# Router logits taken from the residual sums, and the last two tiles of an output projection one after the other

## The chip, the cores and the metric

The kernel runs on one core of a Trainium2 chip. The number that counts is the device time of one execution in microseconds (us): 1569.45 as the median of three runs (1567.67 to 1571.55). The profile is of one more execution, of 1567.72 us.

Five engines work side by side, each through its own queue of instructions, in order, waiting on the others by semaphores: TensorE (PE, matrix products and transposes), VectorE (DVE), ScalarE (ACT), GpSimd (POOL) and SyncE (SP). SP and POOL also issue the transfers between memory and the core.

## What is computed

One encoder layer for 1024 tokens of width 1024, in float32: a token mixer (attention and pooling, merged by gates, with an output projection), a residual sum with layer norm, a mixture of 32 experts of which each token takes two, and a second residual sum with layer norm. The part that matters here:

```
x   = layer_norm(ALPHA * x + merged @ w_out, ln1_gain, ln1_bias)      # 1024 x 1024
g   = x @ w_router_group  + b_router_group                            # 1024 x 4, top 1
e   = x @ w_router_expert + b_router_expert                           # 1024 x 32, top 2 in the group
out = layer_norm(ALPHA * x + sum of two experts, ln2_gain, ln2_bias)
```

An expert is a gated MLP: `(silu(x @ gate) * (x @ up)) @ down`.

## The kernel before

Products are made in three passes of a faster format (`mm3`, lines 161 to 164: high by high, high by low, low by high), so each 128x512 product is three matmul instructions. Around the change there are two stages.

**The output projection.** The 1024 tokens are 8 tiles of 128 rows (0 to 7). `begin` loads a tile's input rows (POOL, line 919) and takes two PSUM banks. A *step* is one call of `mix`: one `k` of eight for one half `n` of the columns, three matmuls (`pw`). After the eight steps of a half, `residual` (lines 931 and 932, VectorE) adds the input and takes the sums for mean and variance; after the second half `norm` (line 936) applies the layer norm in place (`layer_norm`, lines 785 to 798) and writes the rows to memory as `X1`, from which the experts gather.

Between the steps stands the routing of earlier tiles: `turn` (TensorE transposes the rows, `px`; ScalarE copies them, `xT`; POOL scales the rows by ALPHA, line 945, and writes them to `Y`, onto which the experts' results are added), `route` (logits by 8 products against `wr`, line 820, then the choice of group and experts by some 30 small VectorE operations up to `Ms`, line 857), `weights`, `places` (two small products give each token its place in its experts' lists, lines 879 and 880; then one-hots, `ohr`, line 890) and `place` (the one-hots multiplied into the table `first` by two products, line 898). Where each goes is written by hand: `S5` names for each group of tiles the step before which a piece is put, and `S5_END` what comes behind the last step. Tiles 0 and 1 run side by side (a half of 0, a half of 1, and so on), 2 to 5 singly, 6 and 7 side by side. For TensorE and ScalarE this order of the program is kept; VectorE and POOL are ordered by a scheduler.

**The experts.** When all tiles are in the table, VectorE makes the row numbers (`rows_at`, lines 1013 and 1014), POOL gathers rows of `X1` for the first four experts (line 1089), and then TensorE runs through 32 experts. Their weights, 192 pieces of 1 MB, are loaded by SP (line 1048) as soon as one of 15 slots (and a sixteenth buffer) comes free, the first ones during the output projection.

Of the kernel before, what the change touches and what calls it, by code (L numbers as in the profile page):

```python
# [11 lines left out]
F32 = mybir.dt.float32  # L12
# [3 lines left out]
AF = mybir.ActivationFunctionType  # L16
OP = mybir.AluOpType
# [6 lines left out]
D = 1024  # L24
# [30 lines left out]
MEAN_LAG = 1  # L55
B = tuple(2300.0 + 550.0 * i for i in range(8))
FR = (0.5, 0.25, 0.25)
S5_LATE = ((32, "turn", 6),)
S5 = {
    1: (),  # L60
    2: ((13, "turn", 0), (15, "route", 0)),
    3: ((1, "turn", 1), (3, "route", 1), (8, "places", 0), (11, "turn", 2), (13, "place", 0), (13, "route", 2), (14, "places", 1)),
    4: ((2, "place", 1), (4, "places", 2), (10, "turn", 3), (10, "place", 2), (12, "route", 3)),
    5: ((3, "places", 3), (10, "turn", 4), (10, "place", 3), (12, "route", 4)),
    7: ((3, "places", 4), (10, "turn", 5), (10, "place", 4), (12, "route", 5), (21, "places", 5), (26, "place", 5)) + S5_LATE,
}
S5_END = (("logits", 6), ("route", 6), ("turn", 7), ("weights", 6), ("logits", 7), ("route", 7), ("places", 6), ("weights", 7), ("place", 6), ("places", 7), ("place", 7))
Y_OUT = (6, 7)
COMB = ()
M4 = 4  # L70
# [6 lines left out]
C_IOTA, C_FREQ, C_RCNT, C_P, C_DOWN, C_PAY, C_N = 128, 224, 225, 241, 242, 250, 314  # L77


P_GB, P_SUB, P_PS, P_N = 0, 16, 17, 21  # L80


def constants():
# [23 lines left out]
def body(tc, ctx, A, out):  # L107
# [32 lines left out]
    def tiny(shape, name, dt=F32, bufs=2):  # L140
        return (ph["S2"] if "S2" in ph else sm).tile([128] + shape, dt, name=nm(name), tag="t_" + name, bufs=bufs)
# [640 lines left out]
    ps5 = tc.tile_pool(name="ps5", reuse_waits="tile", bufs=1, space=PSUM)  # L782
    p5 = ps5.__enter__()

    def layer_norm(tiny, x, bs, y, g, b):

        mv = tiny([2], "mv")
        DVE.bn_aggr(mv, bs)
        v = tiny([4], "v")
        DVE.tensor_scalar(v[:, 0:1], mv[:, 1:2], EPS, None, op0=OP.add)  # L790
        steps = rsqrt_steps(v[:, 1:2], v[:, 0:1], v[:, 2:3])
        steps[0]()
        DVE.scalar_tensor_tensor(x, x, mv[:, 0:1], g, op0=OP.subtract, op1=OP.mult)
        steps[1]()
        steps[2]()
        DVE.tensor_scalar(v[:, 1:2], v[:, 1:2], -5.0 / 16, None, op0=OP.mult)
        for c in (slice(0, 512), slice(512, 1024)):
            DVE.scalar_tensor_tensor(y[:, c], x[:, c], v[:, 1:2], b[:, c], op0=OP.mult, op1=OP.add)

    wr = ph["S2"].tile([128, 8, 36], F32, name="wr")  # L800
    br = ph["S2"].tile([128, 36], F32, name="br")
    SP.dma_start(wr, A["wr"])
    SP.dma_start(br, bass.AP(tensor=A["br"].tensor, offset=0, ap=[[0, 128], [1, 36]]))

    down8, slots = cst[:, C_DOWN:C_DOWN + 8], cst[:, C_IOTA:C_IOTA + CAP]
    scat = []

    def turned(x):
        xT1 = raw4([8, 128], "xT1")
        for g in range(2):  # L810
            px = p5.tile([128, 4, 128], F32, name=nm("px"), tag="X", bufs=2)
            for k in range(4):
                PE.transpose(px[:, k], x[:, (4 * g + k) * 128:(4 * g + k) * 128 + 128], ident)
            ACT.copy(xT1[:, 4 * g:4 * g + 4], px)
        return xT1

    def logits(xT1):
        pr = p5.tile([128, 512], F32, name=nm("pr"), tag="R", bufs=2)
        for k in range(8):
            PE.matmul(pr[:, :36], xT1[:, k], wr[:, k], start=k == 0, stop=k == 7)  # L820
        lg = tiny([36], "lg")
        DVE.tensor_add(lg, pr[:, :36], br)
        return lg, pr

    def route(j, lg, pr):
# [103 lines left out]
    def residual(j, n):  # L929
        c, x = slice(n * 512, n * 512 + 512), tl[j]["x"]  # L930
        DVE.scalar_tensor_tensor(x[:, c], x[:, c], ALPHA, tl[j]["w"][n], op0=OP.mult, op1=OP.add)
        DVE.bn_stats(tl[j]["s"][:, 6 * n:6 * n + 6], x[:, c])

    def norm(j):
        x = tl[j]["x"]
        layer_norm(tiny, x, tl[j]["s"], x, *lnp)
        POOL.dma_start(X1[j * 128:j * 128 + 128], x)

    def step(what, j):

        if what == "turn":
            x = tl[j]["x"]
            tl[j]["t"] = turned(x)
            y = slot2([D], F32, "yy") if j in Y_OUT else x
            POOL.tensor_scalar(y, x, ALPHA, None, op0=OP.mult)
            POOL.dma_start(Y[j * 128:j * 128 + 128], y)
        elif what == "route":
            if "l" not in tl[j]:
                tl[j]["l"] = logits(tl[j]["t"])
            tl[j]["m"] = route(j, *tl[j]["l"])  # L950
            if j < 6:
                weights(j, *tl[j]["m"][3:])
        elif what == "logits":
            tl[j]["l"] = logits(tl[j]["t"])
        elif what == "weights":
            weights(j, *tl[j]["m"][3:])
        elif what == "places":
            tl[j]["p"] = places(j, *tl[j]["m"][:3])
        else:
            place(j, *tl[j]["p"])  # L960
            if j < 6:
                store_rows(j)


    with tc.manual_schedule(engines={mybir.EngineType.PE, mybir.EngineType.Activation}):
        for group in ((0, 1), (2,), (3,), (4,), (5,), (6, 7)):
            for j in group:
                begin(j)
            todo = list(S5[group[-1]])
            i = 0  # L970
            for n in range(2):
                for j in group:
                    for k in range(8):
                        while todo and todo[0][0] <= i:
                            step(*todo.pop(0)[1:])
                        mix(j, k, n)
                        i += 1
                    if i == 32:
                        for s_ in todo:
                            step(*s_[1:])  # L980
                    residual(j, n)
                    if n:
# [338 lines left out]
def arrange(x, positions, w_in, gate_bias, lam_vecs, subln_gain, w_pool, pool_scale, w_branch_a, w_branch_b, w_out,  # L1321
# [87 lines left out]
```

## Time and profile before

| | |
|---|---|
| median of three runs | 1569.45 us (1567.67 to 1571.55) |
| the profiled execution | 1567.72 us, of which the span of the profile is 1565.9 us |
| busy: PE, DVE, ACT, POOL | 95%, 76%, 60%, 17% of the span |
| output projection, first to last product issued | 809.4 to 921.5 us |
| first gather of the experts | 940.5 us |
| mean granted clock of TensorE | 0.977 of full speed |

Times in a trace count from the start of the span. A matmul's duration includes its way through the pipeline, so back-to-back matmuls overlap; what one costs is read from one start to the next. What stands in brackets at the end of a row is how long the engine was idle before it, and on whom it waited.

### The profile page before, as it was taken

To read this page: it belongs to the slowest core of one execution; us is meant where nothing else is said; L and a number is where in the kernel's file an instruction comes from. 1 tells how busy PE (TensorE), PEld (TensorE's weight loads), DVE (VectorE), ACT (ScalarE), POOL (GpSimd) and SP (SyncE) were. 2 spreads that over 40 slices of the span, in tenths; PEclk is the share of its full clock that TensorE was granted. 3 is DMA by queue.
4 is the path that set the end of the run, shared out by engine and by line. 5 is a ranking of instruction groups with operands and counts; after the bars stand their busy time and mean duration, and the time that the engine had idled before them with its cause. 6 is when DMAs were issued, how large, how long until landed. Compare 5 with 4: busy or idle time off the path is not lost.

```text
span 1565.9 us, 22004 instructions
## 1 busy us (share of the span) xinstructions
PE 1489.4 (95%) x7627; PEld 1190.3 (76%) x7627; DVE 1195.5 (76%) x2284; ACT 945.7 (60%) x1571; POOL 270.0 (17%) x231
## 2 busy tenths in 40 slices
PE   8999999999999999999999987999999999999980
PEld 6988887798798898888888865777777777777750
DVE  5774224987988987775566787999999999899967
ACT  4323124666666666674341125888888888888864
POOL 0001000220210211100002543223222222222110
PEclk9999999999999999999999988999999999999995
DMA  7156223746856755618465568999999999999935
GB/s 235 59 172 203 78 80 96 222 160 168 225 185 182 208 186 145 155 60 315 153 259 196 203 228 291 360 367 378 374 377 370 364 365 364 360 347 368 399 118 215
DMA packets 116977, 375.46 MB, mean 240 GB/s; under 512 B 13767, under 2 KB 44871, under 8 KB 91504
## 3 DMA queue, kind: packets, MB, share of 16 engines
q1 hardware_dynamic: 76128, 303.25, 52.8%
q0 software_dynamic: 40160, 69.96, 17.3%
q8 instruction: 61, 1.00, 0.2%
q10 hardware_dynamic: 576, 0.83, 0.2%
q14 instruction: 52, 0.43, 0.1%
HBM read 312.44 MB, written 69.78 MB: 244 GB/s over the span
## 4 chain that ended last, share of the span: by engine, by line
PE 54%; issue 29%; POOL 9%; DVE 5%; ACT 2%; DMA 2%; POOLq 0%; DVEq 0%; SPq 0%; ACTq 0%
POOL Y L1101 7%; PE ps L570 4%; PE pg L162 4%; PE pg L163 4%; PE pg L164 4%; PE po L621 3%; POOL xg L1089 2%; PE pa L162 2%; PE pa L164 2%; PE pa L163 2%; PE pv L162 2%; PE pv L164 2%; PE tp L606 2%; PE pv L163 2%; PE pw L162 2%
## 5 line engine op out<-in xcount | busy, mean ns | idle before, releaser
L148 DVE TENSOR_TENSOR wh<-we,wh 128x1024 fp32r<-128x1024 f32 x384 | 460.4, 1219 | 57.3 <-ACT wh L147 53.3
L147 ACT CAST wh<-we 128x1024 fp32r<-128x1024 f32 x384 | 401.4, 1046 | 93.4 <-PE gu L164 61.8
L162 PE MATMUL gu<-wh,xT 128*96 128x512 f32 x512 | 204.8, 400 | 1.9 <-ACT xT L147 1.9
L164 PE MATMUL gu<-wh,xT 128*96 128x512 f32 x512 | 203.5, 397 | 0.8 <-DVE xT L148 0.8
L163 PE MATMUL gu<-wh,xT 128*96 128x512 f32 x512 | 202.3, 395 | 0.0
L1101 POOL DMA_INDIRECT Y<-y,idx x32 | 104.6, 3268 | 271.8 <-ACT y L1109 267.0
L148 DVE TENSOR_TENSOR w<-wraw,w 128x512 fp32r<-128x512 f32 x111 | 75.8, 686 | 93.5 <-ACT w L147 93.0
L147 ACT CAST w<-wraw 128x512 fp32r<-128x512 f32 x111 | 68.5, 621 | 115.9 <-PE pg L164 36.4
L573 ACT ACTIVATE P<-ps,stat 128x256 f32<-128x256 f32 (+7 forms) x128 | 94.8, 741 | 59.2 <-DVE stat L572 58.8
L164 PEld LDWEIGHTS gu<-wh,xT 128*96 128x96 f32 x512 | 83.3, 163 | 37.3 <-DVE xT L148 1.5
L162 PEld LDWEIGHTS gu<-wh,xT 128*96 128x96 f32 x512 | 83.4, 163 | 35.3 <-ACT xT L147 2.3
L163 PEld LDWEIGHTS gu<-wh,xT 128*96 128x96 f32 x512 | 83.6, 163 | 34.3 <-issue 0.2
L162 PE MATMUL dn<-wh,hT 128*96 128x512 f32 x256 | 102.5, 400 | 0.6 <-ACT hT L147 0.6
L164 PE MATMUL dn<-wh,hT 128*96 128x512 f32 x256 | 101.0, 395 | 0.0
L570 PE MATMUL ps<-K,Q 128*128 128x512 f32 (+2 forms) x384 | 99.6, 365 | 1.2 <-DVE z L461 0.8
L163 PE MATMUL dn<-wh,hT 128*96 128x512 f32 x256 | 100.6, 393 | 0.0
L162 PE MATMUL pg<-xT,w 128*128 128x512 f32 x256 | 100.5, 393 | 0.0
L163 PE MATMUL pg<-xT,w 128*128 128x512 f32 x256 | 100.1, 391 | 0.0
L164 PE MATMUL pg<-xT,w 128*128 128x512 f32 x256 | 100.0, 391 | 0.0
L572 DVE TENSOR_REDUCE stat<-ps 128x1 f32<-128x256 f32 (+7 forms) x128 | 95.4, 747 | 1.1
L570 PEld LDWEIGHTS ps<-K,Q 128*128 128x128 f32 x384 | 64.7, 189 | 10.8 <-DVE z L461 1.3
L162 PE MATMUL pv<-w,xT 128*128 128x256 f32 x256 | 72.9, 285 | 0.0
(277 smaller groups left out, 3390.6 us busy)
## 6 DMA issues: line engine op xcount, KB each, us to landing
we<-in_we_dram SPq DMA_DIRECT2D x192, 1024.0 KB, 21.7
wraw<-in_w_dram SPq DMA_DIRECT2D x61, 512.0 KB, 3.9
Q<-RQ POOLq DMA_DIRECT2D x64, 256.0 KB, 4.8
RQ<-rh SPq DMA_DIRECT2D x32, 256.0 KB, 3.2
K<-RK POOLq DMA_DIRECT2D x16, 512.0 KB, 4.4
V<-RV POOLq DMA_DIRECT2D x16, 512.0 KB, 5.6
OT<-ohl SPq DMA_DIRECT2D x48, 128.0 KB, 2.4
oT<-OT POOLq DMA_DIRECT2D x6, 1024.0 KB, 10.3
```

The source lines that it names most:

```text
L147: ACT.copy(hi, src)
L148: DVE.tensor_sub(lo, src, r(hi))
L162: PE.matmul(ps, a[0], b[0], start=start, stop=False)
L163: PE.matmul(ps, a[0], b[1], start=False, stop=False)
L164: PE.matmul(ps, a[1], b[0], start=False, stop=stop)
L570: PE.matmul(ps[:, c:c + n], q[:, o, m, qc], Kt[h, m][:, c:c + n], start=o == 0, stop=o == 1)
L572: DVE.tensor_reduce(st_[:, m:m + 1], ps[:, :W], AX.X, OP.max, negate=True)
L573: ACT.activation(Pt[h, i][m][:, :W], ps[:, :W], AF.Exp, bias=st_[:, m:m + 1], accum_out=st_[:, 2 + m:3 + m])
L606: PE.transpose(ps[:, k], p[:, (4 * g + k) * 128:(4 * g + k) * 128 + 128], ident)
L621: PE.matmul(o[:, 0, c], Vt[h][:, a, kt], aT[kt // 4][:, kt % 4, b, c], start=j == 0, stop=j == len(parts) - 1)
L1089: q = POOL.indirect_dma_start(out=x, out_offset=None, in_=X1, in_offset=IO(ap=idx[:, int(e < NXG), expert[e]:expert[e] + 1], axis=0), boun ...
L1101: q = POOL.indirect_dma_start(out=Y, out_offset=IO(ap=idx[:, 0, expert[e]:expert[e] + 1], axis=0), in_=y, in_offset=None, bounds_check=T - ...
```

## The change

The layer norm of a row is a subtraction of its mean, a product with its root and with the gains, and the biases. A logit is linear in that, so it can be had from the residual sum itself: the product of the sum with router rows multiplied by the gains, less the mean times the column sums of these rows, times the root, plus the column sums of the router rows multiplied by the biases.

- Ahead of the projection POOL fills 128x128 ones (in one of the 15 slots) and makes from each of the eight 128x36 blocks of `wr` one times the gain and one times the bias (`w72`); the gains and biases, by column, come with the small parameter block `par`. A new step `router` has TensorE multiply the ones by these 72 columns, in eight products, put before step 8 of tiles 0 and 1; VectorE takes the two sums over (`wc`, `br`).
- ScalarE scales the row of gains by -5/16 once, instead of a VectorE operation for each tile.
- `turn` transposes the residual sum; `norm`, the write of `X1`, the scaling and the write of `Y` come after it. `stats` makes mean and root; `logits` uses them in two VectorE operations in place of one.
- Tiles 6 and 7 run one by one; `S5` and `S5_END` are new. The first half of tile 7's turn is put before step 10 of its own projection, the second behind it.

The diff, without most of the tables (a name that is not defined in it stands in the kernel above):

```diff
-S5_LATE = ((32, "turn", 6),)
-    7: ((3, "places", 4), (10, "turn", 5), (10, "place", 4), (12, "route", 5), (21, "places", 5), (26, "place", 5)) + S5_LATE,
+    7: ((3, "turn", 6), (5, "place", 5), (6, "route", 6), (10, "half", 7), (15, "places", 6)),
...
-    def layer_norm(tiny, x, bs, y, g, b):
...
+    ACT.activation(lnp[0], lnp[0], AF.Copy, scale=-5.0 / 16)
...
+    wgb = slot([704], F32, "wgb")
+    w72, ones = wgb[:, :576].rearrange("p (k n) -> p k n", k=8), wgb[:, 576:]
+    POOL.memset(ones, 1.0)
+    for k in range(8):
+        g, b = (par[:, P_LN + 8 * i + k:P_LN + 8 * i + k + 1] for i in range(2))
+        POOL.tensor_scalar(w72[:, k, :36], wr[:, k], g, 5.0 / 16, op0=OP.mult, op1=OP.mult)
+        POOL.tensor_scalar(w72[:, k, 36:], wr[:, k], b, None, op0=OP.mult)
+    POOL.tensor_copy(wr, w72[:, :, :36])
+
+    def router():
+
+        pr = p5.tile([128, 512], F32, name=nm("pr"), tag="R", bufs=2)
+        for k in range(8):
+            PE.matmul(pr[:, :72], ones, w72[:, k], start=k == 0, stop=k == 7)
+        DVE.tensor_copy(wc, pr[:, :36])
+        DVE.tensor_add(br, br, pr[:, 36:72])
...
-        DVE.tensor_add(lg, pr[:, :36], br)
+        mean, root = tl[j]["r"]
+        DVE.scalar_tensor_tensor(lg, wc, mean, pr[:, :36], op0=OP.mult, op1=OP.subtract)
+        DVE.scalar_tensor_tensor(lg, lg, root, br, op0=OP.mult, op1=OP.add)
...
+    def stats(j):
+
+        mv, v = tiny([2], "mv"), tiny([3], "v")
+        DVE.bn_aggr(mv, tl[j]["s"])
+        DVE.tensor_scalar(v[:, 0:1], mv[:, 1:2], EPS, None, op0=OP.add)
+        for s_ in rsqrt_steps(v[:, 1:2], v[:, 0:1], v[:, 2:3]):
+            s_()
+        tl[j]["r"] = mv[:, 0:1], v[:, 1:2]
+
     def norm(j):
         x = tl[j]["x"]
-        layer_norm(tiny, x, tl[j]["s"], x, *lnp)
+        mean, root = tl[j]["r"]
+        DVE.scalar_tensor_tensor(x, x, mean, lnp[0], op0=OP.subtract, op1=OP.mult)
+        for c in (slice(0, 512), slice(512, 1024)):
+            DVE.scalar_tensor_tensor(x[:, c], x[:, c], root, lnp[1][:, c], op0=OP.mult, op1=OP.add)
         POOL.dma_start(X1[j * 128:j * 128 + 128], x)
+        y = slot2([D], F32, "yy") if j in Y_OUT else x
+        POOL.tensor_scalar(y, x, ALPHA, None, op0=OP.mult)
+        POOL.dma_start(Y[j * 128:j * 128 + 128], y)
...
+        elif what == "turn":
+            for g in range(int(j == 7), 2):
+                turn(j, g)
+            if j < 7:
+                norm(j)
...
-        for group in ((0, 1), (2,), (3,), (4,), (5,), (6, 7)):
+        for group in ((0, 1), (2,), (3,), (4,), (5,), (6,), (7,)):
...
                     if n:
-                        norm(j)
+                        stats(j)
```

What the change moves, at three places. On TensorE, at the end of the projection of before (`px`: transposes, of tile 6 and then of tile 7; `pr<-wr`: logits; `pr<-Ms`: places; `pr<-ohr`: place):

```order
L164 MATMUL pw_9100<-wo_8147,mg_8063 128x512
L813 MATMUL px_9350<-cst,xx_9092 128x128 x4
L813 MATMUL px_9356<-cst,xx_9092 128x128 x4
L820 MATMUL pr_9382<-wr,xT_9349 128x36 x8
L813 MATMUL px_9426<-cst,xx_9097 128x128 x4
L813 MATMUL px_9432<-cst,xx_9097 128x128 x4
L820 MATMUL pr_9453<-wr,xT_9425 128x36 x8
L879 LDWEIGHTS tri
L879 MATMUL pr_9382<-Ms_9423,tri 128x32
```

and of the changed kernel (`pr_9364` is tile 6's, `pr_9501` tile 7's):

```order
L888 MATMUL pr_9364<-Ms_9406,tri 128x32
L889 LDWEIGHTS one
L889 MATMUL pr_9364<-cum,one 128x32
L163 MATMUL pw_9309<-wo_8147,mg_8063 128x512
L164 MATMUL pw_9309<-wo_8147,mg_8063 128x512
L165 MATMUL pw_9309<-wo_8147,mg_8063 128x512
L821 MATMUL px_9486<-cst,xx_9306 128x128 x4
L907 MATMUL pr_9364<-ohr_9458 96x64 x2
L827 MATMUL pr_9501<-wr,xT_9434 128x36 x8
L888 LDWEIGHTS tri
L888 MATMUL pr_9501<-Ms_9550,tri 128x32
```

Tile 6's turn, logits and places now stand ahead of the last projection products; behind them are half a turn, tile 6's place and tile 7.

On VectorE, in the tile 3 group, ahead of the one-hots of tile 1 (`ohr_8697`), with the routing of tile 2 (`t`, `M`, `s`) around them, before:

```order
L852 TENSOR_REDUCE mx_8654<-big_8668 128x4
L888 SCALAR_TENSOR_TENSOR pt_8705,at_8698<-M_8543,pr_8505 128x32
L841 TENSOR_TENSOR t_8657<-big_8668,mx_8654 128x32
L865 SCALAR_TENSOR_TENSOR eq_8680,s_8648<-mx_8654,G_8652 128x4
L890 TENSOR_SCALAR ohr_8697<-cst,at_8698 128x96
L842 TENSOR_TENSOR t_8657<-t_8657,cst 128x32
L890 TENSOR_SCALAR ohr_8697<-cst,at_8698 128x96
L846 TENSOR_REDUCE f_8655<-t_8657 128x4
```

and now (`ohr_8714`):

```order
L855 TENSOR_REDUCE f_8667<-t_8669 128x4
L880 TENSOR_SCALAR s_8660<-s_8660 128x1
L897 SCALAR_TENSOR_TENSOR pt_8722,at_8715<-M_8529,pr_8490 128x32
L856 TENSOR_TENSOR oh_8668<-t_8669,f_8667 128x32
L881 RECIPROCAL s_8660<-s_8660 128x1
L899 TENSOR_SCALAR ohr_8714<-cst,at_8715 128x96
L864 TENSOR_TENSOR M_8687<-G_8664,oh_8668 128x32
L882 TENSOR_TENSOR cst<-s_8660 128x1
L899 TENSOR_SCALAR ohr_8714<-cst,at_8715 128x96
L866 TENSOR_TENSOR Ms_8690<-M_8687 128x32
```

The one-hots have moved from the middle of tile 2's routing to its end, one row ahead of its result `Ms_8690`.

On VectorE behind the last projection product, tile 7 (`xx_9306` are its rows, `lg_9510` its logits), in the changed kernel:

```order
L940 SCALAR_TENSOR_TENSOR xx_9306<-xx_9306,pw_9309 128x512
L912 SCALAR_TENSOR_TENSOR pt_9496,sf_9495<-M_9403,cst 128x32
L941 BN_STATS bs_9310<-xx_9306 128x6
...
L955 SCALAR_TENSOR_TENSOR xx_9306<-xx_9306,mv_9476,lnp_8177 128x1024
L157 TENSOR_TENSOR v_9477<-v_9477 128x1
L157 SCALAR_TENSOR_TENSOR v_9477<-v_9477 128x1
L830 SCALAR_TENSOR_TENSOR lg_9510<-wc,mv_9476,pr_9501 128x36
...
L957 SCALAR_TENSOR_TENSOR xx_9306<-xx_9306,v_9477,lnp_8178 128x512 x2
L838 TENSOR_REDUCE s_9520<-lg_9510 128x1
```

The norm's last two operations stand behind the logits and ahead of the routing that starts with `s_9520`; before, they stood ahead of the transposes.

## Rows read from the trace of the kernel before

**Rows 1.** Windows: length, busy time by engine, granted clock, DMA share.

```profile
851.00:854.40 3.40, 3.40 (x11) 2.82 (x11) 2.74 (x17) 0.39 (x2) 0.50 (x1) 0.50 0.82 269
...
864.00:878.00 14.00, 14.00 (x82) 11.69 (x81) 11.29 (x77) 2.26 (x7) 6.74 (x9) 1.00 0.61 215
...
926.00:940.50 14.50, 7.62 (x36) 6.75 (x36) 13.26 (x98) 5.47 (x11) 3.91 (x3) 0.50 0.51 203
...
985.00:1025.00 40.00, 40.00 (x193) 28.49 (x192) 36.95 (x37) 34.04 (x41) 13.03 (x5) 1.00 1.01 367
```

**Rows 2.** Waits in the expert stage: who for whom, us, times, longest.

```profile
DVE wh L148 <- DMA we<-in_we_dram: 0.2, 1, 0.2
```

**Rows 3.** Timeline of POOL and ScalarE around the projection: start, duration, operation.

```profile
811.09 0.53 POOL L919 DMA_DIRECT2D xx<-in_x_dram  x1 [9.55 <-ACT wo L147]
...
923.60 0.29 ACT L154 ACTIVATE v<-v,rs_b 128x1 f32<-128x1 int32 x1 [0.37 <-DVE v L790]
...
928.04 2.79 POOL L945 TENSOR_SCALAR yy<-xx 128x1024 f32<-128x1024 f32 x1
...
940.53 1.23 POOL L1089 DMA_INDIRECT xg<-X,idx  x1 [8.83 <-ACT wh L147]
```

**Rows 4.** Timeline of VectorE behind the projection, tile 7.

```profile
921.72 0.69 DVE L931 SCALAR_TENSOR_TENSOR xx<-xx,pw 128x512 f32<-128x512 f32 x1 [0.49 <-PE pw L164]
922.44 0.69 DVE L932 BATCH_NORM_STATS2 bs<-xx 128x6 f32<-128x512 f32 x1
...
923.48 1.27 DVE L793 SCALAR_TENSOR_TENSOR xx<-xx,mv,lnp 128x1024 f32<-128x1024 f32 x1
...
925.76 1.41 DVE L798 SCALAR_TENSOR_TENSOR xx<-xx,v,lnp 128x512 f32<-128x512 f32 x2
...
932.07 0.20 DVE L822 TENSOR_TENSOR lg<-pr,br 128x36 f32<-128x36 f32 x1 [0.74 <-PE pr L820]
...
936.02 0.18 DVE L857 TENSOR_TENSOR Ms<-M 128x32 bf16<-128x32 f32 x1
...
939.41 0.29 DVE L1014 SCALAR_TENSOR_TENSOR idx<-first,no 96x32 int32<-96x32 f32 x2
```

**Rows 5.** Timeline of TensorE in the projection.

```profile
809.40 0.39 PE L162 MATMUL pw<-w,mg 128*128 128x512 f32 x1
...
849.41 2.21 PE L820 MATMUL pr<-wr,xT 128*128 128x36 f32 x16 [1.53 <-ACT xT L814]
...
861.67 1.95 PE L820 MATMUL pr<-wr,xT 128*128 128x36 f32 x16 [0.40 <-DVE first L899]
...
882.93 0.18 PE L879 MATMUL pr<-Ms,tri 128*128 128x32 bf16 x1 [0.34 <-DVE Ms L857]
...
897.57 0.18 PE L879 MATMUL pr<-Ms,tri 128*128 128x32 bf16 x1 [0.30 <-DVE Ms L857]
...
902.60 1.03 PE L813 MATMUL px<-cst,xx 128*128 128x128 f32 x8
...
905.24 1.87 PE L820 MATMUL pr<-wr,xT 128*128 128x36 f32 x16
...
921.05 0.40 PE L163 MATMUL pw<-wo,mg 128*128 128x512 f32 x1
921.28 0.39 PE L164 MATMUL pw<-wo,mg 128*128 128x512 f32 x1
```

**Rows 6.** POOL's groups by form: busy, mean ns; its smallest wide operation.

```profile
L520 POOL IOTA io<- 128x128 f32 x1 | 0.3, 269 | 0.1
```

**Rows 7.** Timelines of POOL and VectorE where a POOL scaling runs.

```profile
846.59 2.76 POOL L945 TENSOR_SCALAR xx<-xx 128x1024 f32<-128x1024 f32 x1 [1.78 <-PE px L813]
...
847.30 0.37 DVE L841 TENSOR_TENSOR t<-big,mx 128x32 f32<-128x32 f32 x1
...
927.78 1.37 DVE L850 SCALAR_TENSOR_TENSOR big<-oh,lg 128x32 f32<-128x32 f32 x1
...
929.34 1.52 DVE L884 TENSOR_SCALAR ohr<-M,cst 128x32 f32<-128x32 f32 x1
```

More of the change, by code (lines that the diff above doesn't have):

```diff
@@ L57 @@
 FR = (0.5, 0.25, 0.25)
-S5_LATE = ((32, "turn", 6),)
 S5 = {
[L60 to L64, printed above, removed]
-    7: ((3, "places", 4), (10, "turn", 5), (10, "place", 4), (12, "route", 5), (21, "places", 5), (26, "place", 5)) + S5_LATE,
+    1: ((8, "router", 0),),
+    2: ((3, "turn", 0), (5, "turn", 1), (8, "route", 0), (11, "route", 1)),
+    3: ((2, "places", 0), (3, "turn", 2), (6, "place", 0), (7, "route", 2), (9, "places", 1), (13, "place", 1), (15, "places", 2)),
+    4: ((3, "turn", 3), (5, "place", 2), (6, "route", 3), (15, "places", 3)),
+    5: ((3, "turn", 4), (5, "place", 3), (6, "route", 4), (15, "places", 4)),
+    6: ((3, "turn", 5), (5, "place", 4), (6, "route", 5), (15, "places", 5)),
+    7: ((3, "turn", 6), (5, "place", 5), (6, "route", 6), (10, "half", 7), (15, "places", 6)),
 }
-S5_END = (("logits", 6), ("route", 6), ("turn", 7), ("weights", 6), ("logits", 7), ("route", 7), ("places", 6), ("weights", 7), ("place", 6), ("places", 7), ("place", 7))
+S5_END = (("turn", 7), ("place", 6), ("logits", 7), ("norm", 7), ("route", 7), ("weights", 7), ("places", 7), ("place", 7))
 Y_OUT = (6, 7)
@@ L77 @@
 C_IOTA, C_FREQ, C_RCNT, C_P, C_DOWN, C_PAY, C_N = 128, 224, 225, 241, 242, 250, 314
-P_GB, P_SUB, P_PS, P_N = 0, 16, 17, 21
+P_GB, P_SUB, P_PS, P_LN, P_N = 0, 16, 17, 21, 37
 def constants():
@@ L783, in body @@
     p5 = ps5.__enter__()
-    def layer_norm(tiny, x, bs, y, g, b):
[L787 to L798, printed above, removed]
+    ACT.activation(lnp[0], lnp[0], AF.Copy, scale=-5.0 / 16)
@@ L800, in body @@
     wr = ph["S2"].tile([128, 8, 36], F32, name="wr")
     br = ph["S2"].tile([128, 36], F32, name="br")
+    wc = ph["S2"].tile([128, 36], F32, name="wc")
     SP.dma_start(wr, A["wr"])
     SP.dma_start(br, bass.AP(tensor=A["br"].tensor, offset=0, ap=[[0, 128], [1, 36]]))
+    wgb = slot([704], F32, "wgb")
[5 more added lines that the diff above has]
+        POOL.tensor_scalar(w72[:, k, 36:], wr[:, k], b, None, op0=OP.mult)
@@ L805, in body @@
+    POOL.tensor_copy(wr, w72[:, :, :36])
[5 more added lines that the diff above has]
+        DVE.tensor_add(br, br, pr[:, 36:72])
     down8, slots = cst[:, C_DOWN:C_DOWN + 8], cst[:, C_IOTA:C_IOTA + CAP]
     scat = []
[L808 to L815, printed above, removed]
@@ L817, in logits, with turn @@
-    def logits(xT1):
+    def turn(j, g):
+        x = tl[j]["x"]
+        if "t" not in tl[j]:
+            tl[j]["t"] = raw4([8, 128], "xT1")
+        px = p5.tile([128, 4, 128], F32, name=nm("px"), tag="X", bufs=2)
+        for k in range(4):
+            PE.transpose(px[:, k], x[:, (4 * g + k) * 128:(4 * g + k) * 128 + 128], ident)
+        ACT.copy(tl[j]["t"][:, 4 * g:4 * g + 4], px)
+    def logits(j):
         pr = p5.tile([128, 512], F32, name=nm("pr"), tag="R", bufs=2)
         for k in range(8):
-            PE.matmul(pr[:, :36], xT1[:, k], wr[:, k], start=k == 0, stop=k == 7)
+            PE.matmul(pr[:, :36], tl[j]["t"][:, k], wr[:, k], start=k == 0, stop=k == 7)
@@ L932, in residual @@
         DVE.bn_stats(tl[j]["s"][:, 6 * n:6 * n + 6], x[:, c])
+    def stats(j):
[5 more added lines that the diff above has]
+        tl[j]["r"] = mv[:, 0:1], v[:, 1:2]
     def norm(j):
         x = tl[j]["x"]
-        layer_norm(tiny, x, tl[j]["s"], x, *lnp)
+        mean, root = tl[j]["r"]
+        DVE.scalar_tensor_tensor(x, x, mean, lnp[0], op0=OP.subtract, op1=OP.mult)
+        for c in (slice(0, 512), slice(512, 1024)):
+            DVE.scalar_tensor_tensor(x[:, c], x[:, c], root, lnp[1][:, c], op0=OP.mult, op1=OP.add)
         POOL.dma_start(X1[j * 128:j * 128 + 128], x)
+        y = slot2([D], F32, "yy") if j in Y_OUT else x
+        POOL.tensor_scalar(y, x, ALPHA, None, op0=OP.mult)
+        POOL.dma_start(Y[j * 128:j * 128 + 128], y)
     def step(what, j):
[L941 to L946, printed above, removed]
+        if what == "router":
+            router()
+        elif what == "half":
+            turn(j, 0)
+        elif what == "turn":
[3 more added lines that the diff above has]
+                norm(j)
+        elif what == "norm":
+            norm(j)
         elif what == "route":
             if "l" not in tl[j]:
-                tl[j]["l"] = logits(tl[j]["t"])
+                tl[j]["l"] = logits(j)
             tl[j]["m"] = route(j, *tl[j]["l"])
-            if j < 6:
+            if j < 7:
                 weights(j, *tl[j]["m"][3:])
         elif what == "logits":
-            tl[j]["l"] = logits(tl[j]["t"])
+            tl[j]["l"] = logits(j)
         elif what == "weights":
@@ L1378, in arrange @@
     par[:, P_SUB] = a(subln_gain)[0]
+    for i, v in enumerate((ln1_gain, ln1_bias)):
+        par[:, P_LN + 8 * i:P_LN + 8 * i + 8] = a(v)[0].reshape(8, 128).T
     par[:, P_PS:P_PS + 4] = a(pool_scale)[0].reshape(4, 128).T
```

## The prediction

> **What bounds the kernel now.** I read the table of windows first, then the waits, then the timelines of the output projection, engine by engine. The reader should see three things.
>
> The expert stage is paced by TensorE: in its 40 us windows PE is busy for all 40 [rows 1], and in the whole stage VectorE waits 0.2 us for an expert weight [rows 2]. The weight loads are issued as their slots come free, and the slots come free as the experts use them. So the stage has a fixed length, and the kernel's time moves one for one with the moment at which its first gather can start: POOL at 940.53 [rows 3], right behind the table of rows, which VectorE finishes at 939.41 + 0.29 = 939.70 [rows 4].
>
> Ahead of that lies the output projection, from 809.40 to 921.51 (the last product starts at 921.28 and they follow each other by 0.23) [rows 5]. PE is nearly always busy there. It loses 1.53 + 0.40 + 0.34 + 0.30 = 2.57 us in four waits for ScalarE and VectorE [rows 5], and behind the first of them the granted clock is 0.50 from 851.0 to 854.4, which halves the work of 3.4 us: 1.7 us more [rows 1]. Together 4.3 us.
>
> Last comes a tail in which no projection is left to hide anything: from the residual of tile 7 at 921.72 to 939.70, 17.98 us [rows 4]. It is a chain on VectorE: residual, sums, the norm, then turn, logits and routing of tile 7, with the routing of tile 6 between.
>
> **The change part by part.** All sums are against the profiled execution, 1567.72 us; the median shown, 1569.45, lies 1.73 above it.
>
> *Work moved ahead of the last projection product.* TensorE now does there, too: the logits of tile 6 (1.87 with their pipelined end, 1.7 to the next start), one and a half turns (1.03 each, about 0.9 to the next start: 1.35) [rows 5], the router's eight products, and the two small products of tile 6's places (0.1). The router's products have the same 16 passes as a logits block, with 72 columns instead of 36; their price is between that block's 1.7 and twice that; I take 1.8, since a turn's pass over 128 columns is no dearer than a logits pass over 36. That is +5.0 (4.8 to 6.7). In the kernel before, tile 6's share of it stood in the tail, beside VectorE's norm of tile 7.
>
> *The router's preparation.* POOL fills 128x128 ones and makes 16 small products of 128x36, behind its load of the second input tile, which ends at 811.62 [rows 3]; with the ones that is about 811.9 for the first product. TensorE comes to the router's products after 24 projection products, near 814.9, and needs the last of the sixteen near 816.5. The trace has no POOL operation of that size: the 128x128 iota took 0.27 [rows 6], the 128x1024 scaling 2.79 [rows 3], which by its elements would be 0.1 for 36. At 0.1 to 0.27 each TensorE waits for nothing to 0.3; I take 0.3 and keep 2.0 for a fixed cost that I don't see. The scaling of the gain row on ScalarE stands in front of casts that wait for TensorE anyway, and the slot that the preparation holds is one of the weight slots, all of which are filled before the tail ends: nothing for either. If that cover were gone, it would show as VectorE waiting for a weight.
>
> *The old waits and a new one.* Turning the residual sums instead of the normalised rows frees the turn from some 4 us of VectorE. So I let all of the 4.3 us go. What is late next is VectorE itself in tile 3. From the second residual of tile 2 to the last one-hot of tile 1's places it now has 70 small operations, and the second order listing shows the route of tile 2 in front of that one-hot. In the tail, the 64 rows from 932.07 to 939.41 come to 0.115 each [rows 4]. I count from the start of tile 3: residual and sums 0.7 + 0.7, the norm 1.27 + 1.41 [rows 4] and some 31 small ones end at about 7.6; then it waits for tile 2's logits (8.2) and for tile 3's first half (9.1); residual and sums and 37 small ones end at 14.5. TensorE is there after 13 steps of 0.70, a turn, one place and one logits block, at about 12.5. So it waits some 2 us, up to 3 where a POOL scaling stands in VectorE's way, and the clock fell behind the wait of 1.53 before. I take 1.8 + 1.7 = +3.5 (0.5 if VectorE keeps pace, 5 at worst). Who waits for that: only TensorE; the input of tile 3, which POOL now loads behind two scalings, lands some 2 us ahead of its use.
>
> *The tail.* From the residual's start at 0: residual 0.69, sums to 1.45, their aggregate, place 6's result (a wait that is new here; behind it stand the root and all of tile 7's norm), variance at 2.1; root on ScalarE 2.25 to 2.8 (0.29 for its first half [rows 3]); only behind it, in ScalarE's order, the copy of the second turned half, to 3.35; four logits products to 4.35, two VectorE steps of logits to 5.1, mixed with the norm's first step, which is hidden; the norm's second, 1.41, which VectorE's order puts ahead of the routing, to 6.4; 28 operations of 0.115 to the choice, 9.6; then as now from the choice to the table, 936.02 to 939.70, 3.7: 13.3.
> Beside the routing POOL now scales tile 7's rows (2.8 us from about 7.1). Such a scaling has cost VectorE little (0.37 instead of 0.18 in one operation at 847.30, beside a POOL scaling from 846.59) and much (1.37 and 1.52 where 0.2 is usual, beside the one at 928.04, so about 2.5 in all) [rows 3, 7]. I take 1.5 between these. Tail 14.8 instead of 17.98: -3.2 (-4.5 to -1.5).
> [...]
>
> X1's last write now follows the norm, at about 6.5 after the residual's start; it has until 14.8 to land, so the gather doesn't wait for it.
>
> Sum: +5.0 + 0.3 - 4.3 + 3.5 - 3.2 = +1.3. That is 1569.0 for a profiled execution and **1570.7** for the median.
>
> **The rivals.** A measurement of this kernel can tell about 0.3%, 4.7 us, from no change.
>
> *VectorE keeps pace in tile 3.* For it: it is busy for 11.29 of 14 us in the middle of the projection [rows 1], and the tail's 0.115 includes dependences that interleaving hides. Against: the static order. Then 3.5 becomes 0.5 and the time is 1567.7, still no change that can be told.
>
> *The clock stays up and POOL blocks nothing.* If TensorE's gaps stay short to the end, tile 7's logits and the start of the experts also run at full clock; now the clock is 0.50 from 926.0 on [rows 1]. With no wait in tile 3 (-3.5), no block (-1.3) and about 1.5 of the slow passes back (an estimate: half of some 3 us of logits and first expert products): +1.3 - 6.3 = -5.0, 1564.4, faster. Against: TensorE still stands idle for 5 us in the tail while tile 7 is routed.
>
> *The router's products stall on POOL* (the other side). It decides once a small POOL product takes over 0.29 us (16 of them between 811.9 and 816.5). At 0.6 each the last is ready at 821.7, TensorE waits 5 us less what is due, 3.4 after its own work, and the clock falls behind it (1.7): 5.1 - 0.3 more, 1575.5, slower.
>
> **How the numbers follow.** The forecast 0.55, its variant with the full block 0.08, VectorE in pace 0.16, clock and port 0.09, the router's stall 0.12. Range: with all terms at their low ends 4.8 + 0 - 4.3 + 0.5 - 4.5 = -3.5, 1565.9; at the high ends of all but the router's 6.7, 5.0 + 2.0 - 4.3 + 5 - 1.5 = +6.2, 1575.6. I set 1565 to 1576, which leaves out most of the faster rival. Faster by over 0.3%: that rival and a little of the one in pace, 0.13. Slower: the router's stall and the forecast with its high ends, 0.21. Between: 0.66.
>
> **What would show it.** The last projection product some 4 to 5 us later than 921.28; a wait of TensorE for a one-hot in the fourth group (tile 3) and a dip of the clock behind it; no wait at the router's products; the tail at 14 to 15 us; POOL's last scaling within the routing of tile 7. The prediction is wrong if TensorE has no wait over 1 us in tiles 2 and 3, if the tail is below 13 or above 17, or if the expert stage changes its length.

## The result and the profile after

The changed kernel takes 1579.32 us (median of 6 runs, 1578.47 to 1581.87) against 1568.56 for the kernel before in the same comparison (6 runs): a ratio of 1.0063, with an interval of 1.005 to 1.0076. It is slower by 10.8 us. The prediction, 1570.7 and most likely no change that can be told, was wrong, and its range ended at 1576.

The expert stage is not the cause: in the window that answers to the last of [rows 1] PE is again busy for all of 40 us, and from the first gather to the end of the span it is 625.8 us, before 625.4. So the loss lies ahead of the first gather, which answers to [rows 3]: 951.18 instead of 940.53. From the first projection product to the end of the table of rows it is now 950.35 - 808.60 = 141.75 us, before 939.70 - 809.40 = 130.30. (The part ahead is the same program; in the executions below, all but one, its first product lies between 808.2 and 811.7. In five of them, e1_wide, e2_act, e6_both, e8_place and e11_step8, it is at 810.6 or later, in the eight others at 809.4 or earlier. In e1_wide and e2_act the mean clock from 200 to 300 us is 0.99 and 0.98, long before anything that was changed; in the kernel before, the changed one, e3_fold and e4_single it is 1.00. I therefore compare stretches, not ends; a median can contain such a piece of lower clock too.) The windows of the changed kernel, with the columns of [rows 1]: the router's products, the half clock behind them, the half clock in tile 3, the expert stage.

```profile
814.04:819.96 5.92, 3.60 (x18) 2.54 (x16) 2.45 (x5) 0.09 (x1) 5.92 (x15) 0.92 1.02 426
819.00:822.40 3.40, 3.40 (x10) 2.73 (x11) 0.89 (x3) 0.00 (x0) 1.41 (x4) 0.50 0.99 407
...
871.10:877.00 5.90, 5.87 (x18) 4.48 (x19) 3.16 (x25) 0.00 (x0) 2.59 (x3) 0.50 0.27 102
...
990.00:1030.00 40.00, 40.00 (x190) 28.19 (x189) 36.17 (x39) 33.73 (x42) 11.86 (x5) 1.00 0.99 357
```

TensorE's timeline, to be held against [rows 5]:

```profile
808.60 0.39 PE L163 MATMUL pw<-w,mg 128*128 128x512 f32 x1
...
814.04 0.33 PE L807 MATMUL pr<-wgb 128*128 128x72 f32 x2
815.49 0.44 PE L807 MATMUL pr<-wgb 128*128 128x72 f32 x2 [1.12 <-POOL wgb L800]
...
819.96 0.77 PE L163 MATMUL pw<-w,mg 128*128 128x512 f32 x1
...
871.13 0.93 PE L907 MATMUL pr<-ohr 128*96 128x64 f32 x4 [3.86 <-DVE ohr L899]
...
930.44 0.66 PE L821 MATMUL px<-cst,xx 128*128 128x128 f32 x4 [1.09 <-DVE xx L940]
...
935.04 0.39 PE L165 MATMUL pw<-wo,mg 128*128 128x512 f32 x1
```

From first to last product it is 126.44 us instead of 111.88: +14.56, where the prediction had +4.5 (5.0 + 0.3 - 4.3 + 3.5). Three waits stand out: the router's products for POOL, 3.86 us for tile 1's one-hots in tile 3, and 1.09 for tile 7's residual. Behind the first two the clock is at 0.50 (the second and third of the windows).

POOL's timeline shows the first of them. Its small products take 0.29 and 0.37 us while VectorE stands idle (817.25, 817.60), and up to 1.32 while VectorE splits weights (812.76 to 815.90).

```profile
812.23 0.78 POOL L800 TENSOR_SCALAR wgb<-wr,par 128x36 f32<-128x36 f32 x1
813.00 1.14 POOL L799 TENSOR_SCALAR wgb<-wr,par 128x36 f32<-128x36 f32 x1
814.12 1.32 POOL L800 TENSOR_SCALAR wgb<-wr,par 128x36 f32<-128x36 f32 x1
...
817.25 0.37 POOL L800 TENSOR_SCALAR wgb<-wr,par 128x36 f32<-128x36 f32 x1
817.60 0.29 POOL L799 TENSOR_SCALAR wgb<-wr,par 128x36 f32<-128x36 f32 x1
...
867.21 2.81 POOL L960 TENSOR_SCALAR xx<-xx 128x1024 f32<-128x1024 f32 x1
...
943.54 2.78 POOL L960 TENSOR_SCALAR yy<-xx 128x1024 f32<-128x1024 f32 x1
...
951.18 1.42 POOL L1118 DMA_INDIRECT xg<-X,idx  x1 [3.97 <-ACT wh L148]
```

VectorE's timeline shows the second. Operations of 0.15 to 0.25 us stand there for 1.73 and 1.40, and the first ends at 868.30, 1.09 behind the start of POOL's scaling, the other at 870.06, 0.04 behind its end (870.02). The last four rows are the tail; they answer to [rows 4].

```profile
812.76 3.14 DVE L149 TENSOR_TENSOR wo<-wraw,wo 128x512 fp32r<-128x512 f32 x5
815.82 0.67 DVE L940 SCALAR_TENSOR_TENSOR xx<-xx,pw 128x512 f32<-128x512 f32 x1
...
866.57 1.73 DVE L874 SCALAR_TENSOR_TENSOR eq<-mx,G 128x4 f32<-128x4 f32 x1
...
868.66 1.40 DVE L893 TENSOR_SCALAR ohr<-M,cst 128x32 f32<-128x32 f32 x1
...
870.83 0.25 DVE L899 TENSOR_SCALAR ohr<-cst,at 128x96 f32<-128x96 f32 x1
...
935.47 0.69 DVE L940 SCALAR_TENSOR_TENSOR xx<-xx,pw 128x512 f32<-128x512 f32 x1
...
943.20 1.46 DVE L851 TENSOR_TENSOR t<-t,cst 128x32 f32<-128x32 f32 x1
...
945.54 0.83 DVE L893 TENSOR_SCALAR ohr<-M,cst 128x32 f32<-128x32 f32 x1
...
950.06 0.29 DVE L1043 SCALAR_TENSOR_TENSOR idx<-first,no 96x32 int32<-96x32 f32 x2
```

The tail, from tile 7's last residual to the table, is 950.35 - 935.47 = 14.88 us instead of 17.98.

### The profile page after: what moved, and what is told of

It reads as the page before. It is cut to its first block, busy times and chain, and to the rows that moved or that the text cites. A ratio compares the mean times of both kernels' runs of the same rounds, so it can differ in the third digit from the quotient of the medians.

```text
span 1577.0 us, 22052 instructions
## 1 busy us (share of the span) xinstructions
PE 1493.0 (95%) x7643; PEld 1190.7 (75%) x7643; DVE 1203.5 (76%) x2286; ACT 947.6 (60%) x1572; POOL 281.5 (18%) x249
## 4 chain that ended last, share of the span: by engine, by line
PE 52%; issue 29%; POOL 9%; DVE 7%; ACT 2%; DMA 1%; POOLq 0%; DVEq 0%; SPq 0%; ACTq 0%
POOL Y L1130 7%; PE ps L571 4%; PE pg L163 4%; PE pg L164 4%; PE pg L165 4%; PE po L622 3%; POOL xg L1118 2%; PE pv L163 2%; PE pv L165 2%; PE pv L164 2%; PE tp L607 2%; PE pa L163 2%; PE pa L164 2%; PE pa L165 2%; PE pB L164 2%
## 5 line engine op out<-in xcount | busy, mean ns | idle before, releaser
L571 PEld LDWEIGHTS ps<-K,Q 128*128 128x128 f32 x384 | 64.7, 189 | 10.8 <-DVE z L462 1.3
```

The lines of the kernel that those rows point to most:

```text
L571: PE.matmul(ps[:, c:c + n], q[:, o, m, qc], Kt[h, m][:, c:c + n], start=o == 0, stop=o == 1)
```

## The experiments

All in one table; the stretches are from each profiled execution. The ratios are each against the kernel before in the same comparison, where its median lay between 1567.09 and 1569.36; they aren't the quotients of the medians in the table. A difference between two changed kernels is one between comparisons, and can be off by as much as those medians differ.

| kernel | median us | ratio to before (interval) | first to last product | tail |
|---|---|---|---|---|
| before | 1568.56 | 1 | 111.88 | 17.98 |
| changed | 1579.32 | 1.0063 (1.005 to 1.0076) | 126.44 | 14.88 |
| e1_wide | 1575.90 | 1.0043 (1.0028 to 1.0058) | 120.27 | 14.05 |
| e2_act | 1571.78 | 1.0018 (1.0008 to 1.0028) | 120.54 | 12.30 |
| e3_fold | 1587.25 | 1.0124 (1.0104 to 1.0144) | 127.09 | 20.82 |
| e4_single | 1572.31 | 1.0022 (1.0011 to 1.0034) | 116.36 | 17.21 |
| e5_wide | 1574.11 | 1.0033 (1.002 to 1.0045) | 121.54 | 14.02 |
| e6_both | 1566.61 | 0.9984 (0.9974 to 0.9993) | 114.39 | 12.30 |
| e7_before_act | 1568.58 | 1.0 (0.9991 to 1.0009) | 111.72 | 17.62 |
| e8_place | 1581.31 | 1.0078 (1.0063 to 1.0094) | 123.69 | 14.88 |
| e9_forms | 1573.40 | 1.004 (1.0025 to 1.0055) | 123.25 | 13.76 |
| e10_copy | 1565.79 | 0.9985 (0.9975 to 0.9996) | 116.78 | 11.76 |
| e11_step8 | 1561.30 | 0.9963 (0.995 to 0.9975) | 112.96 | 11.70 |

**The router's stall: e1_wide, e5_wide.** The sixteen small products become two wide ones.

```diff
-    for k in range(8):
-        POOL.tensor_scalar(w72[:, k, :36], wr[:, k], g, 5.0 / 16, ...)
-        POOL.tensor_scalar(w72[:, k, 36:], wr[:, k], b, None, ...)
-    POOL.tensor_copy(wr, w72[:, :, :36])
+    POOL.tensor_mul(w72[:, :, :36], wr, ga)   # ga, be: 8 columns of par,
+    POOL.tensor_mul(w72[:, :, 36:], wr, be)   # each spread over 36
+    POOL.tensor_scalar(wr, w72[:, :, :36], 5.0 / 16, None, op0=OP.mult)   # e5; wc gets the 5/16 too
```

> The sixteen 128x36 products of POOL become two products of 128x288, each tile wide, with the gain's 5/16 put in by ScalarE. Theory A (the router's stall on POOL costs what the trace shows: TensorE needs 5.9 us where its own work is about 2, and runs at half clock for 3.4 us behind it): no wait of TensorE at the router's products, clock 1.00 up to tile 2, last projection product about 5 us earlier than 935.04, and the time about 5 us below the changed kernel, 1574. Rival B (what TensorE gets back here it waits for again later, since VectorE sets the pace in tiles 2 and 3): the wait of 3.86 us for tile 1's one-hots grows by as much, and the time stays within 2 us of 1579. Rival C (POOL's products are slow beside VectorE whatever their number): the two wide ones take several us and the stall stays above 2 us.

> As e1_wide, but the factor 5/16 is put in behind the router's products (in the copy of the column sums, and in POOL's copy of the scaled router rows), so that ScalarE's queue is as in the changed kernel: in e1_wide the extra scaling stood first in ScalarE's order and the first product of the kernel came at 7.86 instead of 6.62. Theory A (the stall at the router is worth what the trace of e1_wide shows between the first projection product and the table of rows, 134.8 us instead of 141.8): the kernel is about 7 us below the changed one, 1572 to 1573. Rival (the rest of e1_wide's gain was lost to something that the wide products bring with them, not to the start): 1575 or more.

In e5_wide TensorE's timeline has no wait there, and the router costs 815.93 - 814.23 = 1.70 us:

```profile
814.23 1.90 PE L806 MATMUL pr<-wgb 128*128 128x72 f32 x16
815.93 0.48 PE L163 MATMUL pw<-w,mg 128*128 128x512 f32 x1
```

```profile
811.17 0.69 POOL L798 TENSOR_TENSOR wgb<-wr,par 128x288 f32<-128x288 f32 x1
811.81 0.68 POOL L799 TENSOR_TENSOR wgb<-wr,par 128x288 f32<-128x288 f32 x1
```

The clock stays at 1.00 behind it (814 to 820 us). The stretch is 4.9 us shorter (e1_wide: 6.2), the time 5.2. That is theory A, somewhat below the 7 expected; B falls (the wait of 3.86 is 3.85, no larger), C falls (the two wide products take 0.69 and 0.68). VectorE's operations stand in the same order as in the changed kernel, so nothing else moved. e1_wide gained only 3.4. Its extra scaling stood first in ScalarE's queue and its first product of all came 1.24 later; its first projection product is 4.1 later, and in that trace the lower clock between 200 and 300 us lies between the two.

**POOL's scaling: e2_act.** `ACT.activation(y, x, AF.Copy, scale=ALPHA)` takes the place of `POOL.tensor_scalar(y, x, ALPHA, ...)`, as a step of its own at 13 of each tile (for tile 1 at 15, for tile 7 behind its weights).

> The 128x1024 scaling of every tile goes from POOL to ScalarE, later in the tile, so that no POOL operation on wide data runs beside VectorE's routing. Theory A (in tile 3 POOL's scaling holds VectorE up by some 2.8 us, two operations of 1.7 and 1.2 instead of 0.2; 0.8 us in tile 7 and 2 us in the tail): TensorE's wait of 3.86 us in tile 3 falls to about 1.1, that of 1.09 for tile 7's first half to about 0.3, the tail from 14.9 to about 13, the time 6 to 9 us below the changed kernel (the more, if the clock no longer falls in tile 3): 1570 to 1574. Rival B (VectorE is late by the number and order of its operations, POOL has little to do with it): the wait in tile 3 stays above 3 us and the time is at most 2 us lower.

TensorE's waits in this kernel from the router to the end of the projection (who for whom, us, times, longest) hold no one-hot any more:

```profile
PE pr L807 <- POOL wgb L800: 2.4, 6, 1.3
PE px L821 <- DVE xx L940: 0.9, 2, 0.8
PE pr L827 <- DVE pt L912: 0.7, 1, 0.7
```

Theory A, and more than it: the wait of 3.86 does not fall to 1.1, it is gone, and the tail is 12.30. 7.5 us of time. Of rival B the number falls: from tile 0's first residual on, the same 185 operations of VectorE stand ahead of tile 1's one-hots as before, and they are in time. Its order is not tested: the scheduler put tile 3's first residual and tile 2's norm at other places among them. So of the 3.86 us the 2.8 that POOL's scaling holds in tile 3 stand in the rows above; whether the other 1.1 came from its earlier holds or from the order, no run separates.

**The form of VectorE's operation: e9_forms.** POOL keeps its scaling; four operations with a column as scalar become operations on two tensors, as `DVE.tensor_tensor(G, tg, fg.to_broadcast([128, 4]), op=OP.is_equal)`.

> The changed kernel, POOL's scaling as it is; the choice of the group, the one-hots and the rows of places are written as operations on two tensors (the column spread over the row) in place of an operation with a column as its scalar. In all traces so far a POOL scaling of 2.8 us holds VectorE twice: one operation up to 1.1 us behind its start, and, where one of these scalar operations comes up later, that one up to POOL's end. Theory F (the second hold hangs on the form of VectorE's operation): no operation of VectorE ends at POOL's end any more, TensorE's wait of 3.86 us in tile 3 falls by about 1.4 to 2.4, the tail by some 0.6, the half-clock stretch stays: 1576 to 1578. Theory G (whatever VectorE runs in the second part of the scaling is held): other operations end at POOL's end, the wait stays at 3.5 to 4 and the time at 1579.

Theory F. POOL's scaling of tile 2 now runs from 867.86 to 870.68, and VectorE has one hold in it, which ends at 868.96, 1.10 behind the start; what follows has its usual length.

```profile
868.00 0.96 DVE L847 SCALAR_TENSOR_TENSOR tg<-lg,s,cst 128x4 f32<-128x4 f32 x1
868.88 0.18 DVE L850 TENSOR_TENSOR t<-lg,mx 128x32 f32<-128x32 f32 x1
...
869.90 0.15 DVE L854 TENSOR_TENSOR G<-tg,fg 128x4 f32<-128x4 f32 x1
```

The wait for the one-hots is 0.61 (another, of 1.71, stands ahead of it at tile 2's logits), the tail 13.76, the time 5.9 lower (4.3 between first product and table), more than expected. Here too the scheduler ordered VectorE's operations anew, so the times are not the form's alone; the holds are. In this execution POOL's first small product lies right beside the same splits of VectorE as in the changed kernel and stands for 4.87 us, to 816.02, 0.15 behind their end; TensorE waits 2.22 us for it, and the clock is at 0.50 from 816.5 to 826.7:

```profile
811.15 4.87 POOL L799 TENSOR_SCALAR wgb<-wr,par 128x36 f32<-128x36 f32 x1
816.02 0.38 POOL L800 TENSOR_SCALAR wgb<-wr,par 128x36 f32<-128x36 f32 x1
```

```profile
812.77 3.10 DVE L149 TENSOR_TENSOR wo<-wraw,wo 128x512 fp32r<-128x512 f32 x5
815.78 0.69 DVE L940 SCALAR_TENSOR_TENSOR xx<-xx,pw 128x512 f32<-128x512 f32 x1
```

**Asking later: e8_place.** `(13, "place", 1)` of tile 3 becomes `(1, "place", 1)` of tile 4.

> The changed kernel, with one step of the schedule moved: tile 1's place from step 13 of tile 3 to step 1 of tile 4; POOL keeps its scaling. Theory A (VectorE's one-hots are ready 3.9 us after TensorE asks for them, because POOL's scaling holds VectorE up): the wait of 3.86 and the half clock behind it, 3 us, go, since TensorE now asks some 7 us later: about 6.8 us below the changed kernel, 1572 to 1573. Rival (VectorE is late for good from tile 3 on): TensorE waits at the next step that needs VectorE, tile 2's places or tile 3's turn, by 3 us or more, and the time stays above 1576.

Mostly the rival. TensorE waits 2.93 us for tile 2's choice instead, and 1.67 instead of 1.09 in tile 7; the clock doesn't fall in tile 3 (1.00 from 874 to 884 us).

```profile
874.39 0.18 PE L888 MATMUL pr<-Ms,tri 128*128 128x32 bf16 x1 [2.93 <-DVE Ms L866]
```

Its stretch is 2.75 shorter in the trace, about the half clock that it doesn't have; its first product comes 2.5 later. Its runs lie among those of the changed kernel (1578.89 to 1582.38): no gain in time can be told. A step moved later does not remove work that VectorE still owes.

**The parts alone: e3_fold, e4_single.** e3_fold has the folded logits, but groups and step table of the kernel before (with the router's products); e4_single takes tiles 6 and 7 one by one, with the old norm and no router.

> Only the first part of the change: logits from the residual sums with the norm folded in, the router's products as in the changed kernel, but tiles 6 and 7 side by side and the steps at the places of the kernel before. Theory A (the loss is the router's stall and the place of tile 1's one-hots in the new schedule): the stall at the router stays (about 5 us with the half clock), the wait for the one-hots is small since this schedule asks for them later, and the tail is some 2 us shorter than 17.98: about 1572 to 1574. Rival D (the fold itself loads VectorE or TensorE more than it gives, wherever the steps stand): 1578 or more.

> Only the second part of the change: tiles 6 and 7 one by one, with the norm ahead of the turn as in the kernel before and no router's products; tile 6's steps stand where tile 5's stand in their tile. By the sum of the prediction the moved work costs TensorE some 3 us (logits and a turn of tile 6), and the tail loses tile 6's routing of some 3 us: within 3 us of the kernel before, 1566 to 1572. If instead taking tiles one by one is what costs (less cover for VectorE in the last tile), there is a new wait in tile 7 and the time is 1575 or more.

e3_fold misses, at 1587, as rival D said by its number, but for a reason of its places. A tile's logits stand right behind its turn there. ScalarE takes its work in the written order, and ahead of the copies of tile 1's turned half stands the exponential for tile 0's routing weights (L878), which waits for VectorE. Its timeline:

```profile
854.09 0.30 ACT L840 ACTIVATE eg<-lg,s 128x4 f32<-128x4 f32 x1 [5.00 <-DVE s L838]
...
858.23 0.30 ACT L878 ACTIVATE s<-s 128x1 f32<-128x1 f32 x1 [3.75 <-DVE eq L873]
```

TensorE waits 4.27 for that copy, and 4.29 for tile 7's in the tail (20.82). So the fold costs time without the new table, which turns a tile three steps ahead of its logits; the router's stall is in these 18.7 us too, since the sixteen small products are. e4_single is 3.8 above the kernel before, not within 3: its products take 4.5 longer, of which some 1.7 are a half clock of 6.8 us at 850.2 where the kernel before has 3.4, and in the tail TensorE waits 5.13 for the norm of tile 7 ahead of the turn, so that it is only 0.8 shorter. The costs of the two parts (18.7 and 3.8) don't add up to the whole (10.8).

**Does the scaling alone help? e7_before_act.** The kernel before with the same edit as e2_act.

> The kernel before, with nothing but the scaling of the tiles moved from POOL to ScalarE. [...] If the scaling on POOL is what the kernel before loses in tiles 2 and 3 as well (its wait of 1.53 and the half clock behind it): 1562 to 1564, and a version that beats both would owe more to the scaling than to the change.

A miss: 1.0000, where I had expected the tail 2 to 2.5 us shorter and 1566. The two held operations of [rows 7] in the old tail lie beside TensorE's turn and logits of tile 7, for which VectorE waits anyway (the logits come at 932.07 [rows 4]); the tail is 0.36 shorter. The null is also a sum: two waits of TensorE for VectorE [rows 5] are gone, and its first wait for ScalarE, which now has the scaling ahead of that copy, grew from 1.53 to 2.28.

```profile
849.56 0.64 PE L820 MATMUL pr<-wr,xT 128*128 128x36 f32 x4 [2.28 <-ACT xT L814]
```

The reading that fits: the scaling costs only where VectorE is what the others wait for, and that the change brought about.

**Versions that beat both: e6_both, e10_copy, e11_step8.** e6_both is e5_wide and e2_act together. e10_copy computes tile 7's statistics one step behind its turn, so that ScalarE copies first. e11_step8 adds the forms of e9_forms and puts `(8, "route", 2)` and `(10, "places", 1)` in place of 7 and 9.

> e5_wide and e2_act together: the router's preparation in wide products, the scaling of the tiles on ScalarE. Theory A (two stalls that are independent of each other, about 7 and 8.5 us between the first projection product and the table of rows): 141.8 - 15.5 = 126.3 us there, 4 us less than in the kernel before (130.3), and the time 1564 to 1566. Rival (one of the two only uncovers the next wait of VectorE in tiles 2 and 3): 130 us or more there, 1568 or more.

> e6_both with one more step moved: ScalarE copies the second half of tile 7's turn ahead of the root of tile 7's variance, not behind it. In e6_both TensorE waits 0.54 us for that copy before the last logits. If those lie on the tail's path: tail 0.5 to 0.9 us shorter than 12.3, and the time 1565.5 to 1566.5, which the measurement can hardly tell from e6_both. If the root is what VectorE needs first: tail unchanged or longer.

> e10_copy with two small edits: VectorE's four scalar operations as in e9_forms (with the scaling on ScalarE they are held by nothing, so at most 0.05 us each), and tile 2's logits one step of 0.70 later in tile 3 (step 8, and tile 1's places at 10). In e10_copy TensorE waits 0.73 us for VectorE at these logits and runs at half clock for 6.8 us behind that wait. If the clock falls because of this wait: no wait over 0.2 us from the first projection product to the last, clock 1.00 up to the tail, some 4 us less, 1562 to 1564. If the wait is only handed on to the next step (tile 1's places or its one-hots): 1565 to 1566.

The gains do add up: e6_both has 114.39 + 12.30 and 0.43 between the two, 127.12 us, from the first product to the table (126.3 expected). e10_copy has the tail 0.54 shorter, but 2.4 us more in the stretch by a half clock in tile 3 (last section); its time can't be told from that of e6_both. e11_step8 is 5.8 us below the kernel before, a little more than expected. The wait of 0.73 is in part handed on: one of 0.68 is left, at tile 2's places, where none over 0.2 was expected. In its windows over the projection the clock is 1.00 throughout:

```profile
811.00:864.00 53.00, 53.00 (x287) 44.99 (x286) 38.53 (x177) 13.68 (x33) 9.78 (x15) 1.00 0.60 231
864.00:870.00 6.00, 5.33 (x30) 4.28 (x29) 5.37 (x37) 2.54 (x5) 1.55 (x2) 1.00 0.98 326
870.00:923.60 53.60, 53.58 (x296) 44.59 (x294) 41.16 (x240) 12.07 (x29) 16.87 (x20) 1.00 0.56 197
```

Its products take 112.96, 1.1 more than before, with 5 us more work in them, and the tail is 6.3 shorter. Whether the moved step keeps the clock up is not shown: in e6_both, without it, the clock is 1.00 there too. Its two edits were not run apart.

## Why the prediction was wrong

- **Moved work, +5.0.** About right. 14.56 less the stalls below and plus the 4.3 of old waits leaves 5.1; e11_step8, with no stall but 0.68, gives 112.96 - 0.68 - (111.88 - 4.3) = 4.7. The router's products are 1.70 (1.8 said).
- **The router's preparation, +0.3. The step that failed first.** I took a POOL product of 36 columns at 0.1 to 0.27 by its elements and by the 0.27 of [rows 6]. It is 0.29 to 0.38 undisturbed, already past the 0.29 from which the rival decides, and up to 1.32 beside VectorE's splits. From 814.04 to 819.96 TensorE needs 5.92 for 1.70 of work; with the rest of its half clock (2.4 us, half of it lost) the stall is 5.4. e5_wide takes it away and gives back 4.9 to 5.2. That is the third rival, by its mechanism and nearly by its price (5.4; it said 5.1); what made the products slow, VectorE beside them, it didn't name. Its chance of 0.12 was too low, since nothing in the trace priced such a product and my bound of 2.0 left the clock out.
- **Old waits, -4.3.** Right: the waits of [rows 5] and the half clock of [rows 1] are gone, but for 0.28 us that I count in tile 3.
- **VectorE late in tile 3, +3.5. The second step that failed, in its cause.** I counted 70 small operations at 0.115 and had VectorE late by some 2. It is not late by its count (e2_act: no wait for one-hots). It is late by POOL's scaling, which holds it for 1.6 and 1.2 us here and has held it beside tiles 0 and 1 before (1.53 and 1.01 in the scaling at 850.79): the wait is 4.3 with its two small neighbours, the half clock costs 2.95 (in this execution it lasts 6.8 us, 0.9 of them within the wait), and VectorE's lateness comes again in tile 7 (1.1; 0.16 in e2_act): 8.4 for 3.5. I had allowed the scaling 1 us here.
- **The tail, -3.2.** Right in sum (14.88 for 14.8), by luck, since its parts are wrong: without POOL's scaling the chain is 12.3, not 13.3 (e2_act). Of the 2.6 between, the scaling costs 1.8, near the 1.5 said: from the start of tile 7's routing to its choice it is 4.74 us here and 2.97 in e2_act. The other 0.84 lies ahead of that, in tile 7's logits, which come 5.08 behind the residual here and 4.24 in e2_act, but 4.23 in e1_wide too, whose tail is 14.05 with POOL's scaling in it. There the last eight logits products take 1.08, here 1.92: here the clock is at 0.50 from 938.5 on, 3.5 behind the last product. That half clock the prediction didn't have. The full block of the variant (0.08) no run shows, nor a port, as a rival's name in the chances has it: the holds that the runs show end at two points (last section).
- **Sum.** 5.1 + 5.4 - 4.3 + 8.4 - 3.1 = +11.5, which is 141.75 - 130.30; it closes because the 5.1 is what the other terms leave. The spans differ by 1577.0 - 1565.9 = 11.1, since the first product came 0.8 earlier here and the rest took some 0.5 longer.

In the first failed step I asked how long a POOL product takes alone, and not what VectorE's splits beside it do. What misled me in the second, and in the tail's price, is a reading: of [rows 7] I took 0.37 us at 847.30 for a case in which POOL's scaling costs VectorE little. That operation started 0.71 behind the scaling's start and ended at 847.67, 1.08 behind it. It was held to the same point as the first hold of the others and had only come late.

## What to carry to other kernels

Beside a wide POOL operation, price VectorE's small ones by where they end, not by how long they take: look for ends that fall together (here 1.1 us behind the start of POOL's operation, and at its end, 2.8). An operation that the trace doesn't show, on an engine that another one can hold, needs the chance of the bad case, and the half clock behind the wait belongs in its price (here 2.95 us behind a wait of 3.86). When a change makes an engine the one that others wait for, what was hidden beside it (here POOL's scaling, worth nothing before and 7.5 us after) comes onto the path.

## What the runs showed of the hardware

- **POOL's scaling holds VectorE at two points.** In the changed kernel's eight scalings from 847.11 on, every VectorE operation that is held ends either 1.08 to 1.11 us behind the start of the scaling or at most 0.07 behind its end (2.8). Up to 1.1 us these are operations on two tensors (in the kernel before a scalar one too, 1.01 us from 859.74); past it only scalar operations with a column, on 128x4 and 128x32 (in e1_wide and e4_single on 128x96 too), and what follows them. Written on two tensors the choice of the group ran through: 0.15 us, 2.04 behind the start (e9_forms). Not every scalar one is held: in the changed kernel those that came up at 1.46 to 1.99 were, three at 1.03 to 1.27 ran at their usual 0.22 to 0.26, and in e3_fold two at 1.29 and 1.54 ran at 0.24 and the next, at 1.68, was held for 1.13. What decides in between stays open. The full block that I set as a variant, VectorE held for a scaling's whole 2.8 us, is not what the rows show: in the scaling at 943.54 VectorE ran eleven operations between its two holds, none longer than 0.22.
- **It goes both ways.** Beside back-to-back splits of VectorE a POOL product of 0.3 us stood for 4.87, until 0.15 behind their end (e9_forms). No run separates how long a single split would hold it.
- **The clock is not told by the wait alone.** Ahead of tile 2's logits TensorE waits 0.73 us in e10_copy and 0.74 in e6_both; behind the first the clock is at 0.50 for 6.8 us, behind the second it stays at 1.00, as it does behind the 2.93 of e8_place. TensorE waited no longer in the one than in the others, and up to tile 7 e10_copy and e6_both have VectorE's and TensorE's operations in the same order: a single trace's half clock is no property of its kernel. What decides stays open. The rows: the wait and the window behind it, of e10_copy, then of e6_both.

```profile
855.50 0.72 PE L826 MATMUL pr<-wr,xT 128*128 128x36 f32 x5 [0.73 <-DVE pt L911]
```

```profile
857.40:860.60 3.20, 3.20 (x11) 2.29 (x11) 2.28 (x21) 0.39 (x2) 1.82 (x3) 0.50 0.82 294
```

```profile
858.90 0.83 PE L826 MATMUL pr<-wr,xT 128*128 128x36 f32 x6 [0.74 <-DVE pt L911]
```

```profile
860.00:866.00 6.00, 5.68 (x31) 4.26 (x31) 5.04 (x43) 0.97 (x4) 2.61 (x3) 1.00 0.84 209
```
